# Another order for VectorE's and ScalarE's work at the entries of the two feed-forward blocks

## The chip, the core and the metric

The kernel runs on one core of a Trainium2 chip. Five engines of the core take their instructions in order, each from its own queue: TensorE (PE in the profile; its weight loads are PEld), VectorE (DVE), ScalarE (ACT), GpSimd (POOL) and SyncE (SP). The metric is the device time of one execution in microseconds (us); the time of a kernel is the median of its timed runs.

## The reference

The reference is a decoder trunk of two layers over 1024 positions of width 1024, in fp32. Layer 0 is a gated short convolution and a SwiGLU feed-forward block; layer 1 is a dilated attention and a second SwiGLU block. Each block is normalised ahead and added to the residual stream:

```
for i in range(DEPTH):
    h = rms_norm(x, mix_norm[i])
    x = x + (short_conv_mixer if i % 2 == 0 else dilated_attention_mixer)(h, ...)
    h = rms_norm(x, ffn_norm[i])
    x = x + (silu(h @ w_gate[i]) * (h @ w_up[i])) @ w_down[i]      # D_FF = 2816
return rms_norm(x, final_norm)
```

The change is about the place where a feed-forward block begins: the norm's statistics (mean of squares, root, reciprocal), the scaled input h, and the first of the products with `w_gate` and `w_up`.

## The kernel before

**Tiles.** The stream is held as 8 tiles X[n] of 128 rows (features) by 1024 columns (positions). Every fp32 operand of a matmul is split into a high part (a copy on ScalarE to fp32r) and a low part (a subtraction on VectorE (L140 for weights, L568 for inputs)), and a product is three matmuls: high by high, high by low, low by high (L575, L576, L577).

**Units and products.** In `Swiglu` a unit u is a pair of weight tiles: even units are gate columns, odd units up columns. Each unit is computed by seven Strassen-Winograd products m = 1, 2, 6, 7, 4, 5, 3, written (u, m) here. A product is 4 k-tiles of 3 matmuls, 12 in all, each of 512 columns. `unit_order` writes the order of the products out by hand. In the second feed-forward block (`key` is 1) it begins, with the place n of each in that list:

```
n:  0 (0,1)  1 (1,1)  2 (2,1)  3 (3,1)  4 (0,2)  5 (1,2)  6 (2,2)  7 (3,2)  8 (4,1)  9 (4,2)
   10 (0,6) 11 (1,6) 12 (0,7) 13 (1,7) 14 (0,4) 15 (1,4) 16 (0,5) 17 (1,5) 18 (0,3) 19 (1,3)
   20 (2,6) 21 (2,5) 22 (2,7) 23 (3,6) 24 (2,4) 25 (2,3) 26 (3,7) 27 (3,5) 28 (3,4) 29 (3,3)
```

In the first block (`key` is 0) it begins (0,1) (1,1) (0,2) (1,2) (2,1) (2,2) (3,1) (3,2) (0,6) (1,6) (0,7) (1,7) (0,4) (1,4) (0,5) (1,5) (0,3) (1,3) (2,6) (2,5) (2,7), n = 0 to 20.

**Banks.** The PSUM pool has 8 banks. A unit's products 1, 6, 7, 4 add up in bank p; product 2 goes to bank q, products 5 and 3 to bank r. After products 1, 6 and 7 `save` copies p to SBUF on ScalarE (L581). `first(u)` adds q to the saved product 1 on VectorE (L585), which ends q's use. Product 4 ends p's use: its result goes straight to `out`. `out` is a Silu on ScalarE for a gate quarter (L1239) and a multiplication on VectorE for an up quarter (L1242). When all four quarters of a pair of units are there, `store` makes four further sums on VectorE (L749), one for each later product.

**Inputs.** b[m] are the four k-tiles of the input for product m, each a page of high and low part. b[1] and b[2] come from `first_half`, made ahead of the block from the left half of the columns. The others come from the right half in `second_half`, a generator that is advanced at given places n: t3 (scale by the norm's factor `rstd`) and b[7]; then t2 = t3 + f and b[6]; then f[4..7] -= t2; then b[4], and h is scaled; then f[0..3] = h - t2; then b[5]; then b[3]. The norm's statistics for the right half are a generator, too: `stats` first issues 8 small matmuls (L485), a root on ScalarE (L488), a reciprocal and a diagonal tile on VectorE (L494), and on its next step two matmuls that spread the factor (L501) and a copy of it on ScalarE (L502).

**Order.** What stands in the program first stands first in its engine's queue. `take` and `ensure` make the weights' parts (L139 copy, L140 subtraction) two products ahead; `ensure(self.at(u, m))` makes them up to that product at once. The weights of products 6, 7, 5 and 3 are sums of raw weight tiles on VectorE (`combos`, L191). SBUF is a pool of 41 pages and one of 20 half pages; a tile that is asked for when none is free waits for the last reader of an earlier one. `feed_forward` runs `start(n)` behind each product n; that is the place where most of the change is.

**Before, in the second block:** n = 0: the last low part of b[2]. n = 1: `combos` of unit 1 and weights up to (0,6). n = 2: statistics, weight (1,6). n = 4: spread, t3, b[7] high parts, the Silu table, weights (0,7) and (1,7). n = 5: `first(0)`, `first(1)`, t2, b[6], low parts of b[7]. n = 6: f[4..7]. n = 11: b[4], h. n = 12: f[0..3]. n = 13: b[5]. n = 16: b[3]. Behind (1,3), n = 19, the first quarters of units 0 to 3 go to `out` together.

Of the kernel before, what the change touches and what calls it, by code (L numbers as in the profile page):

```python
# [13 lines left out]
ALU = mybir.AluOpType  # L14
# [7 lines left out]
KT = D // 128  # L22
# [73 lines left out]
def trunk(ctx: ExitStack, tc: tile.TileContext, x, gains_in, cwi, ck, cwo, wqkv, wo, relb,  # L96
# [444 lines left out]
    class Strassen:  # L541
# [75 lines left out]
        def whole(self, u, m, d):  # L617

            if m == 1:
                d["p"] = self.bank()  # L620
            elif m in (2, 5):
                d["q" if m == 2 else "r"] = self.bank()
            self.mm((u,), m, d["q" if m == 2 else "r" if m in (5, 3) else "p"], m in (1, 2, 5))
            if m in (1, 6, 7):
                d[{1: "u1", 6: "u2", 7: "u3"}[m]] = self.save(d["p"])
            if (u, m) == (0, 6):
                self.first(0)
            if m == 4:
                self.out(u, (1, 0), d.pop("p"))
            elif m == 3:  # L630
                self.out(u, (0, 1), self.add(d.pop("u2"), d.pop("r")))
            elif m in (5, 7) and "u3" in d and "r" in d:
                self.out(u, (1, 1), self.add(d.pop("u3"), d["r"]))
            early = self.key != 0
            if m == 2 and u > 3 + early or (u, m) in ((1, 3) if self.key == 1 else (0, 4), (3, 7)):
                for x in {u * (u < 2): range(4), 3: (4,) * early}.get(u, (u,)):
                    self.out(x, (0, 0), self.first(x))
                    del self.st[x]["u1"]

        def shallow(self, u, m, d):  # L640

# [504 lines left out]
    class Swiglu(Strassen):  # L1146
# [27 lines left out]
        def gained(self, n):  # L1174
# [6 lines left out]
            if n > 3:  # L1181
                self.xd[n - 4] = self.xg[n - 4]
                nc.gpsimd.dma_start(out=self.xd[n - 4], in_=t, accum_op=ALU.add)

        def second_half(self):

            tt = lambda out, a, b, op: nc.vector.tensor_tensor(out=out, in0=a, in1=b, op=op)
            rstd = self.norm.rstd[:, half(1)]
            t3, h, f = self.xd, {k: self.xg[4 + k] for k in range(4)}, self.f
            t2 = {k: X[4 + k][:, half(1)] for k in range(4)}  # L1190
            low7, low = [], None
            for k in range(4):
                tt(t3[k], t3[k], rstd, ALU.mult)
                low7.append(self.hi(7, k, t3[k]))
            if self.key:
                yield
                self.first(0)
                self.first(1)
            for k in range(4):
                tt(t2[k], t3[k], f[k], ALU.add)  # L1200
                nxt = self.hi(6, k, t2[k])
                if low:
                    low()
                low = nxt
            low7.pop(0)()
            low()
            for lo in low7:
                lo()
            yield

            for k in range(4):
                tt(f[4 + k], f[4 + k], t2[k], ALU.subtract)
            yield
            lows = [self.hi(4, k, f[4 + k]) for k in range(4)]
            if self.key:
                for lo in lows:
                    lo()
                lows = []
            for k in range(4):
                tt(h[k], h[k], rstd, ALU.mult)  # L1220
            for lo in lows:
                lo()
            yield
            for k in range(4):
                tt(f[k], h[k], t2[k], ALU.subtract)
            yield
            lows = [self.hi(5, k, f[k]) for k in range(4)]
            for lo in lows:
                lo()
            yield  # L1230
            lows = [self.hi(3, k, h[k]) for k in range(4)]
            for lo in lows:
                lo()
            X[:] = [None] * KT
# [12 lines left out]
        def feed_forward(self, stats, last_step, after, final=None):  # L1247
            prep = []

            def start(n):  # L1250
                if n == 0:
                    last_step()
                    if not self.key:
                        for m in (6, 7):
                            combos[self.key, 1](m)
                        ensure(self.at(3, 1))
                if n == 1 + self.key:
                    next(stats)
                if n == 1:
                    if self.key:  # L1260
                        for m in (6, 7):
                            combos[self.key, 1](m)
                    ensure(self.at(0, 6))
                if n == 2 + 2 * self.key:
                    run(stats)
                    prep.append(self.second_half())
                    next(prep[0])
                    nc.scalar.activation(scratch, eps, AF.Silu)
                if n == 2:
                    ensure(self.at(1, 6))  # L1270
                elif n == 4:
                    ensure(self.at(1, 7))
                if n in ((5, 7, 8, 9, 11), (5, 6, 11, 12, 13, 16))[self.key]:
                    ensure(self.base + n + 3)
                    next(prep[0], None)

            self.run(start)
            key = ("d", self.key)
# [28 lines left out]
    def into_ffn(i, norm):  # L1307
# [49 lines left out]
                       3 if key == "ao" else 4, added=added)  # L1357

        def last_step():
            run(pre[0])  # L1360
            norm.flush()

        return sw, group1, norm.stats(HALF, S), last_step

# [629 lines left out]
```

## Time and profile before

| | |
|---|---|
| time, median of 3 runs | 2137.87 us (2137.76 to 2138.27) |
| the profiled execution | 2138.59 us; span from first to last instruction 2136.8 us |
| granted TensorE clock | 0.998 of full speed |
| TensorE busy | 2117.3 us, 99% of the span |
| VectorE busy | 1718.8 us, 80% |
| ScalarE busy | 992.4 us, 46% |
| GpSimd busy | 221.9 us, 10% |
| first products of the first feed-forward block | from 331.05 us |
| first products of the second feed-forward block | from 1484.73 us |

Times in the traces count from the first instruction of the span. A row of the view of instructions in time order gives the start, the duration, engine, line, operation, tiles and count, and in brackets the idle time of that engine just before, with what ended it. A row of the view of waits gives the waiting engine and line, what it waited for, the total in us, the number of times and the longest. A row of the view by windows gives the window, its length, and for each engine the busy time and the number of instructions. A matmul's shown duration overlaps the next one's, since matmuls are pipelined: two that follow at once start less than one duration apart.

### The profile page before, as it was taken

To read this page: it belongs to the slowest core of one execution; us is meant where nothing else is said; L and a number is where in the kernel's file an instruction comes from. 1 tells how busy PE (TensorE), PEld (TensorE's weight loads), DVE (VectorE), ACT (ScalarE), POOL (GpSimd) and SP (SyncE) were. 2 spreads that over 40 slices of the span, in tenths; PEclk is the share of its full clock that TensorE was granted. 3 is DMA by queue.
4 is the path that set the end of the run, shared out by engine and by line. 5 is a ranking of instruction groups with operands and counts; after the bars stand their busy time and mean duration, and the time that the engine had idled before them with its cause. 6 is when DMAs were issued, how large, how long until landed. Compare 5 with 4: busy or idle time off the path is not lost.

```text
span 2136.8 us, 30748 instructions
## 1 busy us (share of the span) xinstructions
PE 2117.3 (99%) x11086; PEld 1815.5 (85%) x11086; DVE 1718.8 (80%) x3160; ACT 992.4 (46%) x1782; POOL 221.9 (10%) x316
## 2 busy tenths in 40 slices
PE   9999999999999999999999999999999999999998
PEld 7788888888888888878999999888788888888887
DVE  8898769888888888864676767768888888878876
ACT  7433336444544443344545454536544544444435
POOL 2000001111212000010111111110011212100000
PEclk9999999999999999999999999999999999999999
DMA  7222643334545784342333333635125545586432
GB/s 214 69 94 69 237 143 88 124 123 161 180 153 170 262 305 152 108 135 65 88 102 97 103 98 95 205 123 188 33 81 174 168 153 180 172 338 199 156 94 80
DMA packets 149347, 308.82 MB, mean 145 GB/s; under 512 B 50106, under 2 KB 61386, under 8 KB 149194
## 3 DMA queue, kind: packets, MB, share of 16 engines
q1 hardware_dynamic: 83306, 208.92, 30.6%
q0 software_dynamic: 25872, 79.02, 10.5%
q10 hardware_dynamic: 40016, 18.90, 3.0%
q8 instruction: 88, 1.44, 0.3%
q14 instruction: 65, 0.53, 0.1%
HBM read 209.06 MB, written 88.28 MB: 139 GB/s over the span
## 4 chain that ended last, share of the span: by engine, by line
PE 77%; issue 10%; DVE 7%; DMA 3%; ACT 2%; POOL 0%; SPq 0%; DVEq 0%; ACTq 0%; POOLq 0%
PE bank L575 16%; PE bank L577 16%; PE bank L576 16%; PE bank L1584 4%; PE bank L371 4%; PE bank L369 4%; PE bank L370 4%; PE bank L670 2%; PE bank L673 2%; PE bank L672 2%; PE bank L1444 1%; PE bank L1443 1%; PE bank L1442 1%; PE bank L1509 1%; PE bank L1508 1%
## 5 line engine op out<-in xcount | busy, mean ns | idle before, releaser
L575 PE MATMUL bank<-b,w 128*128 128x512 f32 x1816 | 710.0, 391 | 3.8 <-ACT w L139 2.2
L577 PE MATMUL bank<-b,w 128*128 128x512 f32 x1816 | 707.0, 389 | 2.1 <-DVE w L140 2.1
L576 PE MATMUL bank<-b,w 128*128 128x512 f32 x1816 | 707.7, 390 | 0.6 <-DVE b L568 0.3
L575 PEld LDWEIGHTS bank<-b,w 128*128 128x128 f32 x1816 | 341.1, 188 | 77.4 <-ACT w L139 5.2
L577 PEld LDWEIGHTS bank<-b,w 128*128 128x128 f32 x1816 | 341.0, 188 | 74.6 <-DVE w L140 3.4
L576 PEld LDWEIGHTS bank<-b,w 128*128 128x128 f32 x1816 | 341.2, 188 | 71.2 <-DVE b L916 1.1
L139 ACT ACTIVATE w<-combo 128x512 fp32r<-128x512 f32 (+2 forms) x448 | 229.3, 540 | 249.6 <-DVE combo L191 229.7
L140 DVE TENSOR_TENSOR w<-combo,w 128x512 fp32r<-128x512 f32 (+2 forms) x448 | 254.7, 581 | 30.8 <-ACT w L139 30.5
L581 ACT ACTIVATE part<-bank 128x512 f32<-128x512 f32 x168 | 100.2, 597 | 295.9 <-PE bank L577 292.2
L140 DVE TENSOR_TENSOR w<-raw,w 128x512 fp32r<-128x512 f32 (+2 forms) x308 | 169.4, 568 | 23.3 <-ACT w L139 23.1
L585 DVE TENSOR_TENSOR part<-part,bank 128x256 f32<-128x256 f32 (+1 forms) x328 | 154.2, 500 | 35.4 <-ACT part L581 20.0
L139 ACT ACTIVATE w<-raw 128x512 fp32r<-128x512 f32 (+2 forms) x308 | 150.9, 527 | 63.8 <-DMA raw<-in_ffn_w_down 19.1
L831 DVE TENSOR_TENSOR x<-x,bank 128x512 f32<-128x512 f32 x168 | 114.7, 683 | 37.2 <-PE bank L577 34.6
L369 PE MATMUL bank<-w_hi,w 128*128 128x512 f32 (+1 forms) x320 | 119.6, 374 | 0.0
L371 PE MATMUL bank<-w_hi,w 128*128 128x512 f32 (+1 forms) x320 | 117.8, 368 | 0.3 <-DVE w L140 0.3
L370 PE MATMUL bank<-w_lo,w 128*128 128x512 f32 (+1 forms) x320 | 117.7, 368 | 0.0
L506 DVE TENSOR_TENSOR x<-x,bank 128x512 f32<-128x512 f32 (+1 forms) x104 | 66.0, 642 | 56.0 <-PE bank L371 47.0
L369 PE MATMUL bank<-h_hi,w_hi 128*128 128x512 f32 x256 | 104.4, 408 | 0.0
L191 DVE TENSOR_TENSOR combo<-raw 128x512 f32<-128x512 f32 (+1 forms) x160 | 103.2, 645 | 0.0
L371 PE MATMUL bank<-h_hi,w_lo 128*128 128x512 f32 x256 | 100.0, 391 | 0.2 <-DVE w_lo L140 0.2
L370 PE MATMUL bank<-h_lo,w_hi 128*128 128x512 f32 x256 | 99.9, 390 | 0.0
L1603 ACT ACTIVATE z<-bank 64x512 f32<-64x512 f32 x32 | 19.0, 594 | 160.6 <-PE bank L1584 160.4
(266 smaller groups left out, 3816.7 us busy)
## 6 DMA issues: line engine op xcount, KB each, us to landing
hin<-part SPq DMA_DIRECT2D x126, 256.0 KB
raw<-in_ffn_w_gate SPq DMA_DIRECT2D x44, 512.0 KB
raw<-in_ffn_w_up SPq DMA_DIRECT2D x44, 512.0 KB
b<-ready SPq DMA_DIRECT2D x42, 512.0 KB
part<-sum POOLq DMA_DIRECT2D x72, 256.0 KB, 3.5
raw<-in_ffn_w_down SPq DMA_DIRECT2D x48, 384.0 KB
x<-spill SPq DMA_DIRECT2D x24, 512.0 KB
raw<-in_attn_w_qkv SPq DMA_DIRECT2D x24, 512.0 KB
```

What stands on the lines that cost most here:

```text
L139: nc.scalar.activation(hi, src, AF.Copy)
L140: eng.tensor_tensor(out=lo, in0=src, in1=hi, op=ALU.subtract)
L191: eng.tensor_tensor(out=c, in0=a, in1=b, op=op)
L369: nc.tensor.matmul(b, whi[:, a], ahi[:, s], start=first, stop=False)
L370: nc.tensor.matmul(b, whi[:, a], alo[:, s], start=False, stop=False)
L371: nc.tensor.matmul(b, wlo[:, a], ahi[:, s], start=False, stop=last)
L575: nc.tensor.matmul(b, hi[:, a], bhi, start=start and k == 0, stop=False, skip_group_check=True)
L576: nc.tensor.matmul(b, hi[:, a], blo, start=False, stop=False, skip_group_check=True)
L577: nc.tensor.matmul(b, lo[:, a], bhi, start=False, stop=k == n - 1, skip_group_check=True)
L581: nc.scalar.activation(t, b, AF.Copy)
L585: nc.vector.tensor_tensor(out=t, in0=t, in1=b, op=ALU.add)
L831: nc.vector.tensor_tensor(out=X[n][:, half(h)], in0=X[n][:, half(h)], in1=b, op=ALU.add)
```

## The change

In `whole`, unit 0, 1 and 2 of the second block no longer save product 1 right behind it; `start(2)` saves the three together. The first quarters go to `out` in pairs in both feed-forward blocks: those of units 0 and 1 behind (0,4), those of units 2 and 3 behind (2,5); before, all four went behind (1,3) in the second block and behind (0,4) in the first.

In the second block nothing is done at n = 1 any more. At n = 2 the statistics come first, then the three saves, the `combos` of unit 1 and the weights up to (4,2). The spread, t3 and the high parts of b[7] come at n = 3. A new generator `second_later` does the rest: n = 4 `first(0)` and t2; n = 5 `first(1)`, the low parts of b[7], and then the weights (0,6) and (1,6); n = 6 b[6], f[4..7], the scaling of h, and then the weights (0,7) and (1,7); n = 7 f[0..3]; n = 11 b[4]; n = 13 b[5]; n = 15 the high parts of b[3] and two of its low parts; n = 16 the other two.

In `into_ffn`, `last_step` adds the last square to the norm's sum ahead of the last low part of b[2], where it did so behind it. (In the second block that sum is already complete there, so this touches the first block alone.)

No operation is added or removed, and no shape changes.

```diff
--- before.py
+++ after.py
@@ -621,7 +621,7 @@
             elif m in (2, 5):
                 d["q" if m == 2 else "r"] = self.bank()
             self.mm((u,), m, d["q" if m == 2 else "r" if m in (5, 3) else "p"], m in (1, 2, 5))
-            if m in (1, 6, 7):
+            if m in (6, 7) or m == 1 and not (self.key == 1 and u < 3):
                 d[{1: "u1", 6: "u2", 7: "u3"}[m]] = self.save(d["p"])
             if (u, m) == (0, 6):
                 self.first(0)
@@ -632,10 +632,12 @@
             elif m in (5, 7) and "u3" in d and "r" in d:
                 self.out(u, (1, 1), self.add(d.pop("u3"), d["r"]))
             early = self.key != 0
-            if m == 2 and u > 3 + early or (u, m) in ((1, 3) if self.key == 1 else (0, 4), (3, 7)):
-                for x in {u * (u < 2): range(4), 3: (4,) * early}.get(u, (u,)):
-                    self.out(x, (0, 0), self.first(x))
-                    del self.st[x]["u1"]
+            done = {(0, 4): range(4), (3, 7): (4,) * early}
+            if self.key != CONV:
+                done.update({(0, 4): (0, 1), (2, 5): (2, 3)})
+            for x in (u,) if m == 2 and u > 3 + early else done.get((u, m), ()):
+                self.out(x, (0, 0), self.first(x))
+                del self.st[x]["u1"]
 
         def shallow(self, u, m, d):
 
@@ -1182,6 +1184,41 @@
                 self.xd[n - 4] = self.xg[n - 4]
                 nc.gpsimd.dma_start(out=self.xd[n - 4], in_=t, accum_op=ALU.add)
 
+        def second_later(self, low7, t3, t2, h, f, rstd, tt):
+
+            def operand(m, x):
+                for lo in [self.hi(m, k, x[k]) for k in range(4)]:
+                    lo()
+
+            self.first(0)
+            for k in range(4):
+                tt(t2[k], t3[k], f[k], ALU.add)
+            yield
+            self.first(1)
+            for lo in low7:
+                lo()
+            yield
+            operand(6, t2)
+            for k in range(4):
+                tt(f[4 + k], f[4 + k], t2[k], ALU.subtract)
+            for k in range(4):
+                tt(h[k], h[k], rstd, ALU.mult)
+            yield
+            for k in range(4):
+                tt(f[k], h[k], t2[k], ALU.subtract)
+            yield
+            operand(4, {k: f[4 + k] for k in range(4)})
+            yield
+            operand(5, f)
+            yield
+            lows = [self.hi(3, k, h[k]) for k in range(4)]
+            for lo in lows[:2]:
+                lo()
+            yield
+            for lo in lows[2:]:
+                lo()
+            X[:] = [None] * KT
+
         def second_half(self):
 
             tt = lambda out, a, b, op: nc.vector.tensor_tensor(out=out, in0=a, in1=b, op=op)
@@ -1194,8 +1231,8 @@
                 low7.append(self.hi(7, k, t3[k]))
             if self.key:
                 yield
-                self.first(0)
-                self.first(1)
+                yield from self.second_later(low7, t3, t2, h, f, rstd, tt)
+                return
             for k in range(4):
                 tt(t2[k], t3[k], f[k], ALU.add)
                 nxt = self.hi(6, k, t2[k])
@@ -1212,10 +1249,6 @@
                 tt(f[4 + k], f[4 + k], t2[k], ALU.subtract)
             yield
             lows = [self.hi(4, k, f[4 + k]) for k in range(4)]
-            if self.key:
-                for lo in lows:
-                    lo()
-                lows = []
             for k in range(4):
                 tt(h[k], h[k], rstd, ALU.mult)
             for lo in lows:
@@ -1256,23 +1289,29 @@
                         ensure(self.at(3, 1))
                 if n == 1 + self.key:
                     next(stats)
-                if n == 1:
+                if n == 1 + self.key:
                     if self.key:
+                        for u in range(3):
+                            self.st[u]["u1"] = self.save(self.st[u]["p"])
                         for m in (6, 7):
                             combos[self.key, 1](m)
-                    ensure(self.at(0, 6))
-                if n == 2 + 2 * self.key:
+                        ensure(self.at(4, 2))
+                    else:
+                        ensure(self.at(0, 6))
+                if n == 2 + self.key:
                     run(stats)
                     prep.append(self.second_half())
                     next(prep[0])
                     nc.scalar.activation(scratch, eps, AF.Silu)
-                if n == 2:
+                if n == 2 and not self.key:
                     ensure(self.at(1, 6))
-                elif n == 4:
+                elif n == 4 and not self.key:
                     ensure(self.at(1, 7))
-                if n in ((5, 7, 8, 9, 11), (5, 6, 11, 12, 13, 16))[self.key]:
+                if n in ((5, 7, 8, 9, 11), (4, 5, 6, 7, 11, 13, 15, 16))[self.key]:
                     ensure(self.base + n + 3)
                     next(prep[0], None)
+                if self.key and n in (5, 6):
+                    ensure(self.at(1, n + 1))
 
             self.run(start)
             key = ("d", self.key)
@@ -1357,8 +1396,8 @@
                        3 if key == "ao" else 4, added=added)
 
         def last_step():
+            norm.flush()
             run(pre[0])
-            norm.flush()
 
         return sw, group1, norm.stats(HALF, S), last_step
 
```

## The prediction

> **What bounds the kernel now.** I read four views: the page's busy times, the waits of TensorE at the two entries, the windows, and then the instructions in time order around each wait. The page's first part:
>
> ```profile
> PE 2117.3 (99%) x11086; PEld 1815.5 (85%) x11086; DVE 1718.8 (80%) x3160; ACT 992.4 (46%) x1782; POOL 221.9 (10%) x316
> ```
>
> TensorE sets the end, and the change takes no matmul away. It can only shorten stops of TensorE. The waits of TensorE from 1493 to 1560 us (second block), then from 330 to 400 us (first block), and two windows of the second block:
>
> ```profile
> PE bank L577 <- DVE w L140: 1.3, 1, 1.3
> PE bank L501 <- DVE diag L494: 0.8, 1, 0.8
> PE bank L575 <- DVE gate L1242: 0.7, 1, 0.7
> PE bank L575 <- ACT b L567: 0.4, 1, 0.4
> PE bank L576 <- DVE b L568: 0.3, 1, 0.3
> PE bank L575 <- ACT gate L1239: 0.2, 1, 0.2
> ...
> PE bank L577 <- DVE w L140: 0.7, 1, 0.7
> PE bank L485 <- DVE acc L470: 0.4, 1, 0.4
> ...
> 1484.70:1576.40 91.70, 88.01 (x384) 70.73 (x383) 83.88 (x142) 49.22 (x88) 8.91 (x14) 1.00 0.28 91
> 1527.00:1553.00 26.00, 23.15 (x97) 17.66 (x96) 25.14 (x42) 12.47 (x23) 2.77 (x5) 1.00 0.12 51
> ```
>
> Six stops in the second entry, 91.70 - 88.01 = 3.69 us of idle time; two in the first, 0.7 + 0.4 = 1.1. A window's row gives its length and then the busy time of PE, PEld, DVE, ACT and POOL: VectorE has 83.88 of 91.70, and 25.14 of 26.00 in the middle. So VectorE's queue decides what is late, and TensorE what that costs.
>
> Idle time is not the whole loss, as starts show. Two products' first matmuls, and the stop inside (2,7):
>
> ```profile
> 1484.73 0.39 PE L575 MATMUL bank<-b,w 128*128 128x512 f32 x1
> ...
> 1487.46 0.40 PE L575 MATMUL bank<-b,w 128*128 128x512 f32 x1
> ...
> 1550.55 0.39 PE L576 MATMUL bank<-b,w 128*128 128x512 f32 x1
> 1552.20 0.50 PE L577 MATMUL bank<-b,w 128*128 128x512 f32 x1 [1.27 <-DVE w L140]
> 1552.54 0.39 PE L575 MATMUL bank<-b,w 128*128 128x512 f32 x1
> ```
>
> Twelve matmuls take 2.73 us, so 0.227 from start to start, though each is shown as 0.39. Around the stop the starts are 1.65 and 0.34 apart: 1.42 + 0.11 = 1.53 lost, where 1.27 is shown idle. I add 0.26 to every stop: 3.69 + 6 x 0.26 = **5.25 us** in the second entry.
>
> The busy share alone would put the most there is to gain at 3.69 + 1.1 = 4.8 us. The Trainium skill, page "Trainium Kernel Development and Optimization", section "Performance Expectations", calls matmul busy time a bad measure because matmuls are pipelined; the rows above agree (0.39 shown, 0.227 apart). By idle time alone the gain below would be 4.5 us, by starts it is 6.4.
>
> **The change, stop by stop.** No instruction comes or goes, so each term is a stop that ends or moves. I walk ScalarE's and VectorE's queues in the new order, each with its pitch from rows: VectorE 0.60 (a x4 group below takes 2.49, its first result 0.69), ScalarE 0.52, a product 2.72. The same walk in the old order meets the trace's six stops within 0.3 us each.
>
> *The spread.* Statistics, ScalarE's queue ahead of the root, and the diagonal tile:
>
> ```profile
> 1492.91 0.94 PE L485 MATMUL bank<-ones,acc 128*128 128x1 f32 x8
> 1493.72 0.49 PE L575 MATMUL bank<-b,w 128*128 128x512 f32 x1
> ...
> 1493.68 0.71 ACT L1179 ACTIVATE x<-x,gains 128x512 f32<-128x512 f32 x1
> 1494.30 1.06 ACT L581 ACTIVATE part<-bank 128x512 f32<-128x512 f32 x2
> 1495.25 2.19 ACT L139 ACTIVATE w<-raw 128x512 fp32r<-128x512 f32 x4
> 1498.33 0.27 ACT L488 ACTIVATE r<-bank,eps 128x4 f32<-128x4 f32 x1
> ...
> 1499.56 0.69 DVE L494 TENSOR_TENSOR diag<-eye,r 128x512 f32<-128x512 f32 x1
> ```
>
> The sums are there at 1493.85, but the root stands behind saves and weight copies until 1498.33. In the new order it is next on ScalarE, at 1494.3; VectorE has only one low part ahead, so the diagonal tile is done at about 1495.5. TensorE asks for it behind (3,1), at 1493.72 + 2.72 = 1496.4: 0.9 to spare. The 0.8 stop goes. The three saves and four weight copies come behind the root; the first of those weights, for (2,2), is ready at 1498.0 and wanted at 1502.9.
>
> *The two r banks.* Products (0,5) and (1,5) wait for the banks that (0,4) and (1,4) leave:
>
> ```profile
> 1528.54 2.50 ACT L567 ACTIVATE b<-hcol 128x512 fp32r<-128x512 f32 x4 [1.40 <-DVE hcol L1187]
> 1530.94 0.58 ACT L1239 ACTIVATE gate<-bank 128x512 f32<-128x512 f32 x1
> ...
> 1530.83 2.49 DVE L568 TENSOR_TENSOR b<-hcol,b 128x512 fp32r<-128x512 f32 x4
> 1534.44 0.69 DVE L1242 TENSOR_TENSOR gate<-bank,gate 128x512 f32<-128x512 f32 x1
> ```
>
> The Silu stands behind b[5]'s copies, which wait for f on VectorE; the multiplication stands behind b[5]'s low parts. In the new order h is scaled at n = 6 and f made at n = 7, some 8 us sooner, so b[5]'s copies start at 1526.0 as soon as the weight ahead of them. The Silu runs when (0,4) ends, at 1528.0, and frees the bank at 1528.6, wanted at 1530.1. On VectorE b[5] is done at 1529.1; the moved multiplication of unit 1's first quarter, a `combo` and a weight go ahead, and the gate multiplication runs from 1531.1 to 1531.8, wanted at 1532.8. Both stops go, with 1.5 and 1.0 to spare.
>
> *b[3], for (0,3):*
>
> ```profile
> 1538.02 2.18 ACT L567 ACTIVATE b<-x 128x512 fp32r<-128x512 f32 x4
> ...
> 1538.77 2.49 DVE L568 TENSOR_TENSOR b<-x,b 128x512 fp32r<-128x512 f32 x4
> ```
>
> The copies stood behind a Silu that waited for VectorE. One place sooner (n = 15) they run from 1531.2 to 1534.8. Two low parts follow at 1532.9 and 1533.5; the other two stand behind an add of (0,5), two sums and a weight, at 1536.7 and 1537.3. (0,3) would start at 1535.5 and ask for the third low part at 1535.5 + 2 x 0.68 + 0.23 = 1537.1; it is there at 1537.4. Of the two stops one of 0.35 stays, with its tail 0.45.
>
> *The pairs of quarters, for (2,7):*
>
> ```profile
> 1547.54 1.28 DVE L585 TENSOR_TENSOR part<-part,bank 128x512 f32<-128x512 f32 x2
> 1548.92 0.69 DVE L1242 TENSOR_TENSOR part<-part 128x512 f32<-128x512 f32 x1
> ...
> 1551.46 0.69 DVE L140 TENSOR_TENSOR w<-combo,w 128x512 fp32r<-128x512 f32 x1
> ```
>
> (2,7)'s weight stood behind these three and one more multiplication. Now those of units 0 and 1 are over by (0,4), those of 2 and 3 come behind (2,5), after this weight. Its low part runs from 1545.8 to 1546.5, wanted at 1547.3: 0.8 to spare. The moved work delays (2,4)'s weight, done at 1551.6, wanted at 1552.7, and (2,3)'s, done at 1555.3, wanted at 1555.45. **That last 0.15 is what is late next.** Saving units 0 to 2 together costs nothing: their banks p stay in use until product 4 anyway.
>
> *The first block.* The stops are the sum of squares and (1,5)'s weight:
>
> ```profile
> 335.74 0.69 DVE L568 TENSOR_TENSOR b<-hcol,b 128x512 fp32r<-128x512 f32 x1 [0.16 <-ACT b L567]
> 336.35 0.69 DVE L470 TENSOR_TENSOR acc<-acc,sq 128x512 f32<-128x512 f32 x1
> ...
> 372.40 1.28 DVE L585 TENSOR_TENSOR part<-part,bank 128x512 f32<-128x512 f32 x2
> ...
> 374.99 0.68 DVE L140 TENSOR_TENSOR w<-combo,w 128x512 fp32r<-128x512 f32 x1
> ...
> 392.78 0.69 DVE L585 TENSOR_TENSOR part<-part,bank 128x512 f32<-128x512 f32 x1 [1.34 <-ACT part L581]
> ```
>
> With the sum ahead of the low part, TensorE starts the statistics 0.6 sooner: the stop's 0.4 and the 0.16 by which a shown duration passes a pitch (0.39 - 0.227). The diagonal tile there then comes about as TensorE asks for it. Units 2 and 3's adds and multiplication, from 372.40 to 374.39, leave the place ahead of (1,5)'s weight, which is then ready at 373.7, wanted at 374.2. That stop was 0.7 + 0.26 = 0.96. Together **1.6 us**; the three moved operations now stand behind (2,5), where VectorE idles 1.34 us; without that cover an add that no product waits for is 1.9 instead of 0.6 us late.
>
> **Sum.** 5.25 - 0.45 + 1.6 = 6.4 us. The profiled execution took 2138.59 (span 2136.8 and 1.8 around it) and would take 2132.2; it lies 0.7 above the median, 2137.87, so I forecast 2137.87 - 6.4 = **2131.5 us**. The most that can go is 5.25 + 1.6 and a few tenths of uncounted tails, 7.2: 2130.7.
>
> **Rivals.**
>
> *B, a page wait.* b[3] now asks for four pages while the weights of (1,4), (0,5), (1,5) and (0,3) are all alive. I count 24 pages of b, 4 of X, 8 raw weights and those 4: 40 of 41. The second to fourth copies must wait for a reader. Before, that happened at b[6]:
>
> ```profile
> 1514.99 0.63 ACT L567 ACTIVATE b<-x 128x512 fp32r<-128x512 f32 x1 [1.75 <-DVE b L568]
> ```
>
> My walk lets them go with (1,4)'s end and the first two low parts. If they must wait for (1,5)'s end at 1535.6, the next Silu, the weights of (1,3) and (2,6) and VectorE's low parts queue behind: the stop at (0,3) is 1.8 (fourth copy alone) to 3.1 us (from the second on) instead of 0.35, and the time 2133.0 to 2134.2. For it: every page is taken. Against it: earlier readers end in time. In the Trainium skill, "TensorE: Matmul & The Clock Gate", section "Architectural detail", ScalarE's queue is strictly first in, first out, so one waiting copy holds all behind it; the wait of 1.75 above, with nothing overtaking, agrees.
>
> *C, VectorE becomes the bound.* The margins are 0.15 to 1.0, and VectorE idles 0.86 of 26 us in the crowded stretch. Each us that it runs behind my walk from (0,3) on is a us of TensorE. At 2.1, three or four operations, the gain is down to 4.3. I give 2133.6 to 2137. Against it: the old order came out right by the same walk.
>
> *D, slower.* t3 needs accumulating DMAs, and stands ahead of `first(0)` on VectorE:
>
> ```profile
> L1183 POOL DMA_DIRECT2D x<-x x4: 842/850/882, 1487.8 to 1494.7; - x4
> ...
> DMA to landing us min/median/max: 6.9/7.6/8.5
> ```
>
> The last lands at 1494.7 + 6.9 = 1501.6, just when the new order asks for it; the old one asked 2 us later. If landings slip, VectorE holds `first(0)`, which frees the bank that (4,1) takes. That is wanted at 1508.3 and due at 1502.3, so 6 us are hidden, then each costs one; beyond 12.4 us the kernel is slower than before, 2139.5 at 14. Against it: 8.5 is the longest landing.
>
> **Chances.** Forecast 0.60 (2130.7 to 2132.4), B 0.20, C 0.14, D 0.06. What can be told from no change is about 0.2%, 4.3 us: 2133.6. Faster takes the forecast and most of B, 0.76; the same, the rest of B and most of C, 0.18; slower, D, 0.06. The range, 2130.6 to 2134.5, holds the forecast, B and a little of C.
>
> **What would show it.** Right: between 1493 and 1500 no wait of L501 for the diagonal tile; no wait of L575 for L1239 or L1242; no stop in (2,7); one short wait for L568 near 1537; the first block without waits for L470 and L140. (3,6) and what follows start some 6.4 us sooner against the span's start. Wrong: a b<-x copy on ScalarE idle for a us or more near 1532 to 1536 (B); new waits of L577 for L140 at (2,7) to (3,7) (C); VectorE idle at t3 for a DMA (D).

## The result and the profile after

The changed kernel takes **2130.56 us** (median of 6 runs, 2128.91 to 2131.29), the kernel before, timed beside it, 2138.07 (6 runs): 7.5 us less, ratio 0.9964 (95% interval 0.9954 to 0.9974). The forecast was 2131.5 with a range from 2130.6; the time lies 0.04 us below that range, with three of the six runs inside it. The profiled execution took 2130.26 us, its span is 2128.5.

TensorE's work is the same to the instruction, as the counts behind the x in the profile after show:

```profile
PE 2114.2 (99%) x11086; PEld 1815.6 (85%) x11086; DVE 1718.4 (81%) x3160; ACT 991.4 (47%) x1782; POOL 221.8 (10%) x316
```

What went is best read from windows that begin and end at the same matmul in both kernels. Each begins at the first product of a block and is called the block's entry here. The kernel before (window, its length, then busy time and count of PE, PEld, DVE, ACT, POOL; the granted clock; the DMA share and GB/s):

```profile
331.02:401.44 70.42, 69.30 (x305) 56.14 (x304) 66.05 (x112) 38.62 (x68) 6.10 (x10) 1.00 0.31 94
1484.76:1576.40 91.64, 87.95 (x384) 70.70 (x383) 83.82 (x142) 49.16 (x88) 8.91 (x14) 1.00 0.28 91
```

and the changed kernel:

```profile
331.04:399.65 68.61, 68.61 (x305) 56.39 (x304) 65.85 (x111) 38.31 (x68) 6.07 (x10) 1.00 0.33 97
1482.20:1568.70 86.50, 86.50 (x384) 70.94 (x383) 83.23 (x141) 48.82 (x88) 8.88 (x14) 1.00 0.30 96
1524.00:1550.00 26.00, 26.00 (x115) 21.12 (x114) 25.11 (x43) 13.19 (x24) 3.83 (x7) 1.00 0.14 56
```

The same 305 matmuls of the first block take 70.42 - 68.61 = **1.81 us** less, the same 384 of the second 91.64 - 86.50 = **5.14 us** less. (The prediction's window of the second entry, 91.70 us, begins 0.03 us ahead of the first matmul, the two of that entry here 0.03 behind it.) In all three windows after, TensorE is shown busy from end to end. Its busy time fell by 87.95 - 86.50 = 1.45 us in the second entry though no matmul went, so a part of the stops was shown as busy time. VectorE still has 25.11 of 26.00 us in the crowded stretch: it does the same work, in an order that shows no idle time of TensorE.

ScalarE of the changed kernel in time order, at the spread, and then at the Silu that frees an r bank and at b[3]:

```profile
1491.75 0.24 ACT L488 ACTIVATE r<-bank,eps 128x4 f32<-128x4 f32 x1
1491.89 1.56 ACT L581 ACTIVATE part<-bank 128x512 f32<-128x512 f32 x3
...
1525.41 0.59 ACT L1272 ACTIVATE gate<-bank 128x512 f32<-128x512 f32 x1
...
1528.47 0.61 ACT L567 ACTIVATE b<-x 128x512 fp32r<-128x512 f32 x1
1529.68 0.63 ACT L567 ACTIVATE b<-x 128x512 fp32r<-128x512 f32 x1 [0.59 <-DVE combo L191]
1530.53 1.15 ACT L567 ACTIVATE b<-x 128x512 fp32r<-128x512 f32 x2 [0.22 <-PE bank L577]
```

VectorE of the same kernel, from the spread to the pair of quarters:

```profile
1492.23 0.69 DVE L494 TENSOR_TENSOR diag<-eye,r 128x512 f32<-128x512 f32 x1
...
1528.36 0.68 DVE L1275 TENSOR_TENSOR gate<-bank,gate 128x512 f32<-128x512 f32 x1
...
1533.90 1.28 DVE L568 TENSOR_TENSOR b<-x,b 128x512 fp32r<-128x512 f32 x2
...
1542.92 0.69 DVE L140 TENSOR_TENSOR w<-combo,w 128x512 fp32r<-128x512 f32 x1
...
1544.72 1.28 DVE L585 TENSOR_TENSOR part<-part,bank 128x512 f32<-128x512 f32 x2
```

The root is the first thing on ScalarE behind the statistics, the three saves (L581) follow it. The pair of additions (L585) now stands behind (2,7)'s weight (L140 at 1542.92). b[3]'s second and third copies each wait a little (0.59 and 0.22), and its last two low parts come at 1533.90. That is where the one trace of a stop is left, inside (0,3):

```profile
1534.35 0.39 PE L575 MATMUL bank<-b,w 128*128 128x512 f32 x1
1534.64 0.50 PE L576 MATMUL bank<-b,w 128*128 128x512 f32 x1
1534.97 0.39 PE L577 MATMUL bank<-b,w 128*128 128x512 f32 x1
```

The starts are 0.29 and 0.33 us apart where 0.227 is the pitch (the time from start to start when nothing is awaited), and no idle time is shown: a stop of less than 0.39 - 0.227 = 0.16 us is hidden in the shown duration of the matmul ahead of it.

### The profile page after: what moved, and what is told of

It is laid out like the page before. It is cut to its first block, busy times and chain, and to the rows that moved or that the text cites. A ratio compares the mean times of both kernels' runs of the same rounds, so it can differ in the third digit from the quotient of the medians.

```text
span 2128.5 us, 30749 instructions
## 1 busy us (share of the span) xinstructions
PE 2114.2 (99%) x11086; PEld 1815.6 (85%) x11086; DVE 1718.4 (81%) x3160; ACT 991.4 (47%) x1782; POOL 221.8 (10%) x316
## 3 DMA queue, kind: packets, MB, share of 16 engines
q8 instruction: 88, 1.44, 0.3%
## 4 chain that ended last, share of the span: by engine, by line
PE 95%; DVE 3%; ACT 1%; issue 1%; DMA 0%; DVEq 0%; ACTq 0%
PE bank L575 19%; PE bank L576 19%; PE bank L577 19%; PE bank L371 6%; PE bank L369 6%; PE bank L370 6%; PE bank L1623 5%; PE bank L672 2%; PE bank L675 2%; PE bank L674 2%; PE bank L1483 1%; PE bank L1482 1%; PE bank L1481 1%; PE bank L1548 1%; PE bank L1547 1%
## 5 line engine op out<-in xcount | busy, mean ns | idle before, releaser
L140 DVE TENSOR_TENSOR w<-combo,w 128x512 fp32r<-128x512 f32 (+2 forms) x448 | 254.4, 581 | 29.7 <-ACT w L139 29.5
L581 ACT ACTIVATE part<-bank 128x512 f32<-128x512 f32 x168 | 100.1, 597 | 295.4 <-PE bank L577 290.4
L140 DVE TENSOR_TENSOR w<-raw,w 128x512 fp32r<-128x512 f32 (+2 forms) x308 | 169.2, 568 | 22.8 <-ACT w L139 22.6
L585 DVE TENSOR_TENSOR part<-part,bank 128x256 f32<-128x256 f32 (+1 forms) x328 | 154.1, 500 | 33.3 <-ACT part L581 18.0
L191 DVE TENSOR_TENSOR combo<-raw 128x512 f32<-128x512 f32 (+1 forms) x160 | 103.1, 645 | 0.0
```

Source lines behind the costliest of these rows:

```text
L140: eng.tensor_tensor(out=lo, in0=src, in1=hi, op=ALU.subtract)
L191: eng.tensor_tensor(out=c, in0=a, in1=b, op=op)
L585: nc.vector.tensor_tensor(out=t, in0=t, in1=b, op=ALU.add)
```

## The experiments

In each profile the window that holds the same 384 matmuls of the second entry is quoted; its length is compared with the 86.50 us above. Each window begins and ends some 0.03 us behind the start of the same matmul, so that the length does not move with what happens elsewhere in the execution. "L" numbers are those of the kernel in question.

**The same kernels once more**, no edit.

> The changed kernel, not altered. Theory: the sum of the prediction was too small at its terms (1.8 us for the first block, 5.2 for the second by the starts of the first profiles), and what lies outside the two entries is variation between executions: the ratio to the kernel before is 0.9962 to 0.9970, 8.1 to 6.4 us, and in this profile the second entry is left with one stop of 0.2 to 0.4 us, while the stop of 757 us and the last transfers come out either way. Rival: the change also takes away work outside the entries; then the stop at 757 us is gone and the last transfers land some 9.7 us behind the last matmul here too.

> The kernel before, not altered, for a second profile. Theory: in the two entries the same stops as in the first profile within 0.3 us each (3.7 us idle from 1484 to 1577, 1.1 from 330 to 400); the stops elsewhere (0.26 us at 757 us, the start of the kernel, the last transfers at 10.5 us behind the last matmul) may come out otherwise, by some tenths of a us. Rival: they come out as in the first profile; then they belong to the old order and their loss is the change's.

Measured: the changed kernel 2130.43 (2130.15 to 2130.6), ratio 0.9965 (0.9951 to 0.9979); the kernel before as an experiment of its own 2137.09 (11 runs), beside 2137.72 (24 runs) for the very same kernel timed as the comparison: 0.63 us apart. The windows of the changed kernel:

```profile
331.26:399.87 68.61, 68.61 (x305) 56.38 (x304) 65.84 (x111) 38.32 (x68) 6.05 (x10) 1.00 0.32 97
1483.09:1569.57 86.48, 86.48 (x384) 70.94 (x383) 83.21 (x141) 48.81 (x88) 8.87 (x14) 1.00 0.30 96
```

The kernel before, the same two windows:

```profile
331.31:401.69 70.38, 69.28 (x305) 56.14 (x304) 66.04 (x112) 38.62 (x68) 6.09 (x10) 1.00 0.31 94
1483.95:1575.65 91.70, 87.93 (x384) 70.69 (x383) 83.83 (x142) 49.16 (x88) 8.90 (x14) 1.00 0.28 91
```

The entries repeat within 0.06 us (the second gives 91.70 - 86.48 = 5.22 this time), the rest does not. The stop for a raw weight near 757 us is in the first profile of before, not in the second; it is not in the first profile of the changed kernel, which has one near 1907 us instead, and is back in its second. The waits, each row with who waited for what, the total, times and longest; the kernel before, first profile, from 750 to 760 us:

```profile
PE bank L575 <- ACT w L139: 0.3, 1, 0.3
```

The changed kernel, first profile, from 1900 to 1918 us:

```profile
PE bank L575 <- ACT w L139: 0.6, 1, 0.6
```

The changed kernel, second profile, from 750 to 760 us:

```profile
PE bank L575 <- ACT w L139: 0.5, 1, 0.5
```

So these stops come and go in both orders, and the rival that the change takes them away falls. Behind the last matmul before had 8.2 and 8.0 us to the end of the span, the changed kernel 7.25 and 7.4, the first block's part alone 7.0. All twelve profiles of kernels with the change or a part of it lie between 6.9 and 7.5, so some 0.5 us or more may have gone there; whether that has to do with the order stays open.

**One block alone.** The first kernel is the kernel before with the first block's part only:

```
-            if m == 2 and u > 3 + early or (u, m) in ((1, 3) if self.key == 1 else (0, 4), (3, 7)):
-                for x in {u * (u < 2): range(4), 3: (4,) * early}.get(u, (u,)):
...
+            done = {(1, 3) if self.key == 1 else (0, 4): range(4), (3, 7): (4,) * early}
+            if self.key == 0:
+                done.update({(0, 4): (0, 1), (2, 5): (2, 3)})
...
         def last_step():
-            run(pre[0])
             norm.flush()
+            run(pre[0])
```

> Only the first block's part of the change, on the kernel before: the sum of squares ahead of the low part, and the quarters in pairs. Theory: 1.6 us (prediction) to 1.8 us (starts in the profile after) faster than before, ratio 0.9991 to 0.9993, with the second entry's six stops as before. Rival, that the first block's gain is lost again further on: ratio 1.0000.

The second is the changed kernel with these two put back:

```
-            if self.key != CONV:
+            if self.key == 1:
                 done.update({(0, 4): (0, 1), (2, 5): (2, 3)})
...
-            norm.flush()
             run(pre[0])
+            norm.flush()
```

> Only the second block's part of the change; the first block as before. Theory: 4.8 us (prediction) to 5.2 us (starts) faster than before, ratio 0.9976 to 0.9978, and with the other part alone it adds up to the whole change within 0.5 us. Rival, that the two parts need each other or that the second block gives more than its own stops: 6 us or more, ratio 0.9972 or less.

Measured: 2134.64 (ratio 0.9986, 0.9977 to 0.9995) and 2131.98 (0.9973, 0.9963 to 0.9983). The first and second entry of the first block's part alone:

```profile
330.99:399.60 68.61, 68.61 (x305) 56.38 (x304) 65.86 (x111) 38.32 (x68) 6.07 (x10) 1.00 0.33 97
1482.04:1573.71 91.67, 87.94 (x384) 70.71 (x383) 83.85 (x142) 49.20 (x88) 8.90 (x14) 1.00 0.28 91
```

The second block's part alone:

```profile
330.99:401.39 70.40, 69.30 (x305) 56.14 (x304) 66.04 (x112) 38.63 (x68) 6.09 (x10) 1.00 0.32 94
1484.37:1570.90 86.53, 86.53 (x384) 70.95 (x383) 83.11 (x141) 48.84 (x88) 8.86 (x14) 1.00 0.30 96
```

By the windows the parts are independent: the first gives 70.42 - 68.61 = 1.81 and leaves the second entry at 91.67, the second gives 91.64 - 86.53 = 5.11 and leaves the first at 70.40. The medians give 3.1 and 5.7, whose sum, 8.8, misses the whole, 7.3, by more than the 0.5 us expected. With 0.6 us between two timings of one kernel, and intervals of 2 us on each side, a part of this size cannot be sized by medians.

**The root back behind its queue**, the spread left early. The diff is against the changed kernel, second block:

```
-                    next(stats)
-                if n == 1 + self.key:
                     if self.key:
                         for u in range(3):
...
                         ensure(self.at(4, 2))
-                    else:
+                    next(stats)
+                    if not self.key:
                         ensure(self.at(0, 6))
```

> The changed kernel, with the root, its reciprocal and the diagonal tile of the second block put back behind the three saves, the two sums of products and the four weights, while the spread stays asked for one product sooner. Theory of the prediction: the root starts behind 3 saves of 0.48 and 4 copies of 0.52, about 3.5 us later than now, the diagonal tile is done near 1499 us on the axis of before and wanted at 1496.4: one stop of 2.4 to 3.0 us at L501, and 2.6 to 3.3 us slower than the changed kernel (2133.0 to 2133.8). Rival, that the early root matters little because later slack takes the delay up: under 1 us.

Measured: 2134.58 us (2132.33 to 2135.71; 0.9987, 0.9978 to 0.9996). The first matmul of the spread, in time order:

```profile
1497.05 1.22 PE L501 MATMUL bank<-diag,ones 128*128 128x512 f32 x1 [3.02 <-DVE diag L494]
```

The entry and three windows across the stop:

```profile
1482.05:1574.57 92.52, 89.50 (x384) 72.59 (x383) 83.25 (x141) 49.07 (x88) 8.85 (x14) 0.96 0.28 90
...
1495.00:1495.98 0.98, 0.00 (x0) 0.00 (x0) 0.98 (x2) 0.84 (x3) 0.00 (x0) 1.00 1.09 238
1495.98:1502.81 6.83, 5.76 (x12) 3.90 (x13) 3.48 (x7) 2.89 (x5) 0.00 (x0) 0.50 0.25 48
1502.81:1505.00 2.19, 2.19 (x11) 1.79 (x10) 1.31 (x3) 2.16 (x5) 0.00 (x0) 1.00 0.00 0
```

The stop came at the place and in the size expected, 3.0 us. The loss did not: 92.52 - 86.50 = 6.0 us, twice the expected 2.6 to 3.3. The windows show why: while TensorE stood, its granted clock fell to 0.50 at 1495.98, 1.95 us into the idle time (1497.05 - 3.02 = 1494.03), and came back at 1502.81, 5.76 us after work had begun again. So the place of the root alone decides over the spread's stop, the rival falls, and this stop costs about twice its length. Beside the kernel before (2137.18) the median is 2.6 us less, where the unaltered changed kernel has 7.3: 4.7 us lost. The ten runs lie 3.4 us apart; whether all lost as much to the clock as the profiled one is not shown.

**The scalings back** (h behind b[4]'s low parts, f just ahead of b[5]):

```
                 tt(f[4 + k], f[4 + k], t2[k], ALU.subtract)
+            yield
+            yield
+            operand(4, {k: f[4 + k] for k in range(4)})
             for k in range(4):
                 tt(h[k], h[k], rstd, ALU.mult)
...
                 tt(f[k], h[k], t2[k], ALU.subtract)
-            yield
-            operand(4, {k: f[4 + k] for k in range(4)})
-            yield
             operand(5, f)
```

> The changed kernel, with h scaled again behind b[4]'s low parts and f made again just ahead of b[5]. Theory: the bank stops come back, 0.4 us at (0,5) and 1.4 at (1,5), and the stop inside (0,3) grows to 1.2: about 2.8 us slower than the changed kernel (2133.2). Rival, that the pages or VectorE as a whole bind and the place of the scalings does not: no stop at (0,5) and (1,5), under 0.5 us.

The entry's window:

```profile
1482.76:1572.16 89.40, 87.44 (x384) 70.73 (x383) 82.96 (x141) 49.17 (x88) 8.85 (x14) 1.00 0.29 94
```

Its waits of TensorE there:

```profile
PE bank L575 <- ACT gate L1272: 0.7, 1, 0.7
PE bank L575 <- ACT b L567: 0.7, 1, 0.7
PE bank L576 <- DVE b L568: 0.6, 1, 0.6
```

2132.64 us; the entry is 2.90 longer (expected 2.8), with the three stops at the three places named; they share the loss more evenly than expected (0.7 at (0,5) and at (1,5) instead of 0.4 and 1.4, and 0.6 shown inside (0,3) instead of 1.2). The moved scalings are thus what cleared both r banks and most of (0,3).

**Three moves undone one at a time:** the quarters in one place behind (1,3); the spread one product later; b[3] all at n = 16.

```
-            if self.key != CONV:
+            if self.key == 1:
+                done = {(1, 3): range(4), (3, 7): (4,)}
+            elif self.key != CONV:
                 done.update({(0, 4): (0, 1), (2, 5): (2, 3)})
```

```
-                if n == 2 + self.key:
+                if n == 2 + 2 * self.key:
                     run(stats)
```

```
             operand(5, f)
             yield
-            lows = [self.hi(3, k, h[k]) for k in range(4)]
-            for lo in lows[:2]:
-                lo()
             yield
-            for lo in lows[2:]:
+            lows = [self.hi(3, k, h[k]) for k in range(4)]
+            for lo in lows:
                 lo()
```

> The changed kernel, with the second block's four quarters again in one place behind (1,3). Theory: (2,7)'s weight comes 2.5 us later on VectorE, of which 1.0 is slack: one stop of 1.4 to 1.6 us for that weight at (2,7) and 1.1 us slower in all, since a small stop at (0,3) goes (2131.6). Rival: under 0.4 us, if the other moves have already made enough room.

> The changed kernel, with the spread and the t3 products one product later, as in the kernel before; the root stays ahead. Theory: the root's place alone takes the stop away, and what follows has the room; no stop of L501, within 0.3 us of the changed kernel (2130.2 to 2130.8). Rival: the earlier spread is what gives the later operands their room; new stops of 0.5 us or more at (0,6) to (0,4).

> The changed kernel, with all of b[3] made one place later, as in the kernel before. Theory: the copies stand again behind the Silu of (0,5), and (0,3) stops for 0.6 us instead of 0.2 to 0.35: 0.3 us slower at most, too little for the time to tell; the profile shows a stop at L575 or L576 for b of 0.5 to 0.8 us. Rival: the stop is 1 us or more, as before (0.4 + 0.3 with tails 1.2).

The entry with the quarters back:

```profile
1482.59:1570.12 87.53, 86.51 (x384) 71.03 (x383) 83.80 (x142) 48.83 (x88) 8.88 (x14) 1.00 0.30 95
```

The spread later:

```profile
1483.95:1570.45 86.50, 86.50 (x384) 70.95 (x383) 83.05 (x141) 48.89 (x88) 8.87 (x14) 1.00 0.30 97
```

b[3] later:

```profile
1483.22:1570.05 86.83, 86.50 (x384) 71.04 (x383) 83.25 (x141) 48.45 (x88) 8.87 (x14) 1.00 0.30 96
```

They are 1.03, 0.00 and 0.33 us longer, against 1.1, 0 and up to 0.3 expected. The first stops 1.0 us for (2,7)'s weight (1.4 to 1.6 expected), the third 0.3 inside (0,3) (0.5 to 0.8 expected). The second shows that the earlier spread by itself brings nothing here. The medians are 2130.27, 2129.55 and 2130.21, which is 6.9, 7.6 and 7.2 us below the kernel before timed beside each; the unaltered changed kernel is 7.3 below. A loss of 1.03 us shows there as 0.4, one of 0.33 as 0.1, and none as a gain of 0.3: differences under 1 us stand in the windows alone. (In all three profiles the clock fell for 3.4 us near 937 us, far from these edits; the last section has it.) The place of the three saves was not undone by itself.

**Rival B, one page less.** A tile that is written and read once holds one page from n = 4 to n = 20 of the second block:

```
+                if self.key and n == 4:
+                    self.held = [page("held") for k in range(1)]
+                    for t in self.held:
+                        nc.gpsimd.memset(t[:, :8], 0.0)
+                if self.key and n == 20:
+                    for t in self.held:
+                        nc.gpsimd.tensor_copy(self.kept, t[:, :8])
+                    del self.held
```

> The changed kernel, with one page of the on-chip memory held by an extra tile from the fifth to the twenty-first product of the second block. Rival B of the prediction, that pages bind at b[3]: the copies of b[3] or b[5] wait for a reader, and a stop of 0.5 to 2.8 us at (0,3) or sooner shows. Theory (one page of 41 is free): the ScalarE copies wait somewhat longer and TensorE shows at most 0.3 us more.

The entry of this kernel:

```profile
1484.39:1571.77 87.38, 86.79 (x384) 70.87 (x383) 83.26 (x141) 48.95 (x88) 9.20 (x16) 1.00 0.29 96
```

ScalarE there, at b[3]:

```profile
1532.54 1.15 ACT L567 ACTIVATE b<-x 128x512 fp32r<-128x512 f32 x2 [1.44 <-DVE combo L191]
```

0.88 us longer, with a stop of 0.6 inside (0,3): more than the theory's 0.3, at the low end of rival B's 0.5 to 2.8. The first copy of b[3] now waits 1.44 us, until a `combo` on VectorE (L191) ends, for a page where in the changed kernel it was the second, for 0.59. The rival's mechanism is real and one page away; in the changed kernel it stays off TensorE's path. (The median, 2133.19, is higher than this explains; in this profile the first block's entry began at 332.0 us, in all others between 330.7 and 331.5, and took 0.5 us more than in the changed kernel; VectorE waited 2.5 us instead of 1.5 for accumulating transfers of the sums of squares (L470), shortly before and in it. The edit does not touch that place; why it happened there is not known.)

**Rival C, VectorE's room.** Additions of 128x64 on a small tile, ahead of b[3]'s last two low parts, 6 of them (shown) or 14:

```
+            for k in range(6):
+                tt(self.spare, self.spare, self.spare, ALU.add)
             for lo in lows[2:]:
                 lo()
```

> The changed kernel, with six small additions on VectorE (128x64, some 0.14 to 0.2 us each, about 1 us together) ahead of the last two low parts of b[3]. Theory: there is no slack on VectorE at (0,3): the stop inside (0,3) grows by the sum of the six, to 1.0 to 1.5 us, and what follows keeps its margin because TensorE is as much later. 0.8 to 1.2 us slower than the changed kernel. Rival: 0.5 us or more of it is taken up by slack.

> The same with fourteen additions (about 2.2 to 2.8 us). Theory: one stop of 2.2 to 3.0 us inside (0,3) and no other; 2.0 to 2.8 us slower than the changed kernel, linear with the six. Rival C of the prediction, that VectorE is the bound from there on: stops at (2,7), (2,4) or (2,3) too, and more than 3.2 us slower.

The entry with six:

```profile
1484.02:1571.94 87.92, 86.59 (x384) 70.94 (x383) 84.38 (x147) 48.76 (x88) 8.87 (x14) 1.00 0.29 94
```

VectorE there, the six and what follows:

```profile
1535.70 1.52 DVE L1229 TENSOR_TENSOR spare<-spare 128x64 f32<-128x64 f32 x6
1537.13 1.28 DVE L568 TENSOR_TENSOR b<-x,b 128x512 fp32r<-128x512 f32 x2
```

The low parts are 1537.13 - 1535.70 = 1.43 us later, and the entry is 1.42 us longer (somewhat over the expected 0.8 to 1.2, since one addition took 0.24 rather than 0.14 to 0.2). There is no slack at this place, and no other stop follows. With fourteen, the entry and two windows from the stop on:

```profile
1482.92:1574.21 91.29, 87.88 (x384) 72.07 (x383) 86.91 (x156) 48.98 (x88) 8.88 (x14) 0.98 0.29 92
...
1538.00:1538.44 0.44, 0.00 (x0) 0.00 (x0) 0.44 (x2) 0.00 (x0) 0.00 (x0) 1.00 0.00 0
1538.44:1541.86 3.42, 2.99 (x7) 2.42 (x8) 3.32 (x6) 0.00 (x0) 0.54 (x1) 0.50 0.00 0
```

4.79 us longer, over the 2.0 to 2.8 expected of the theory and over the 3.2 named for rival C. Yet rival C's sign, stops at (2,7), (2,4) or (2,3), is absent: the one stop inside (0,3) is 3.41 us long, since an addition took 0.25, and the clock fell again, at 1538.44, for 3.0 us of work, which makes up most of the rest (4.79 - 3.41 - 0.16 = 1.2). VectorE binds at (0,3) alone. The medians, 2131.75 and 2135.79, agree in direction (1.6 and 5.6 us lost, each against the kernel before beside it).

## Why the prediction was right and wrong

**The stops: right.** The signs it named are there: no wait for the diagonal tile, for the Silu or the gate multiplication, none in (2,7), none in the first block for L470 or L140. Only the short wait for L568 inside (0,3) is too short to be shown as one, and (3,6), named to start some 6.4 us sooner, starts 7.7 sooner in the first pair of profiles and 6.1 in the second. In times, too, the walk of the two queues holds. The second entry's axis after lies 2.55 us ahead of before's; shifted by that, the forecast has the diagonal tile done at 1492.95 (it is 1492.92), the Silu at 1525.45 (1525.41), the gate multiplication at 1528.55 (1528.36), b[3]'s first copy at 1528.65 (1528.47), its last low parts from 1534.15 (1533.90), (2,7)'s weight from 1543.25 (1542.92).

**The step that failed is the sum with its ceiling,** "The most that can go is 5.25 + 1.6 and a few tenths of uncounted tails, 7.2: 2130.7". The stops did not exceed that ceiling: the entries gave 6.95 us. It failed as the bound of a measured time, since the sum put all that lies outside the entries at nothing, without a reason. Two of its terms were small, and that third one missing:

- *The first block:* 1.6 predicted, 1.81 measured. By starts 0.5 of it went at the statistics, as priced, the rest at (1,5). The stop there was priced at its idle time and 0.26. But a second stop follows in that product that shows no idle at all. TensorE of the kernel before:

```profile
377.90 0.39 PE L577 MATMUL bank<-b,w 128*128 128x512 f32 x1
378.22 0.47 PE L575 MATMUL bank<-b,w 128*128 128x512 f32 x1
378.53 0.40 PE L576 MATMUL bank<-b,w 128*128 128x512 f32 x1
```

Starts 0.32 and 0.31 apart, 0.17 us over two pitches, with nothing in the brackets.

- *The second block:* 5.25 - 0.45 = 4.8 predicted, 5.14 measured (5.22 in the second pair of profiles). The stop that was to stay at (0,3), "with its tail 0.45", cost 0.18 there and 0.14 more at the start of the next product, 0.32 in all by the starts. What the six stops had cost was thus 5.14 + 0.32 = 5.46, where 3.69 + 6 x 0.26 = 5.25 was put: 0.30 beyond its idle time for each, instead of 0.26. (With the scalings put back, three stops of 0.69, 0.68 and 0.59 cost 2.90 + 0.32 in all, 0.42 each beyond their idle time, but that includes a delay at the start of (0,3) that shows no idle time.)

Together 6.95 us instead of 6.4. From the median used, 2137.87 - 6.95 = 2130.92, which would have lain inside the range.

- *Nothing outside the entries.* The measured 7.5 and 7.3 us are 0.6 and 0.3 more than the two entries give in the same pair of profiles. The forecast had no term for this, and its lower bound left it no room. Two timings of one kernel differ by 0.63 us, and stops for raw weights of 0.3 to 0.6 us come and go in both orders; that is enough for the difference, so it need not be the change's. How much of it is, stays open. (A fall of the clock near 937 us, 1.6 us in size, is in the profiles of four variants and in none of these two kernels' four; whether any of their other runs had it is not known.) That the median came to lie just below the edge, and not just above, was chance: of the six runs three lie on either side.

**The rivals.** B was put as "The second to fourth copies must wait for a reader". They did wait, for 0.81 us, and TensorE hardly noticed; with a page less it did. C asked for VectorE to run behind the walk; it ran ahead of it by 0.2 to 0.3 us. Of the narrow margins, (2,3)'s "last 0.15" held too. D, late landings of the accumulating transfers, was not tried on the chip. In the changed kernel t3 followed the weights at 1497.18, but the last transfer, issued at 1492.1, landed 6.9 us later at the soonest, at 1499.0, as the fourth of the scalings came up; the four took 2.59 us, in the kernel before 2.50. So D's landings came as just in time as it said, and its 6 us of room on TensorE's side were not touched.

## What to carry to other kernels

Where one engine sets the end and its stops are waits for results of other in-order queues, walk those queues in the new order with durations from the rows, and read both the stop and the gain from starts of the same instruction, since shown idle time misses every stop shorter than the pipelined overlap (0.16 us here). Do not set the edge of a range at the sum of the stops that one profile shows: leave it the spread between two timings of one kernel, 0.6 us here. A change of some tenths of a per cent is sized by equal-work windows of two profiles, which begin at the start of the same matmul, not by medians.

## What the hardware showed that was not expected

A stop of TensorE had two prices here. Up to the 1.3 us of the six additions the loss was the delay of the awaited result (1.42 for 1.43 us). At 3.0 and 3.4 us the granted clock fell to half within the stop, 1.95 us into the idle time in the one case and 2.98 in the other (1538.87 - 3.41 = 1535.46, and 1.00 until 1538.44), and stayed there for 5.76 and 2.99 us of work. From fall to return that is 6.83 and 3.42 us. Matmuls then started 0.427 us apart instead of 0.227. A stop of 1.5 to 1.6 us near 62 us, which every profile has, left the clock at 1.00, and none has a stop between that and 3.02 us, so where the second price begins is not shown. TensorE of the kernel with fourteen additions:

```profile
1538.87 0.80 PE L576 MATMUL bank<-b,w 128*128 128x512 f32 x1 [3.41 <-DVE b L568]
1539.46 0.63 PE L577 MATMUL bank<-b,w 128*128 128x512 f32 x1
1539.89 0.63 PE L575 MATMUL bank<-b,w 128*128 128x512 f32 x1
```

The Trainium skill, page "TensorE: Matmul & The Clock Gate", section "Part 1: The HAM clock gate (the "warmup" mystery)", describes this: the array's clock is halved once an activity window of about 3.4 us has passed idle, the window runs free of the kernel, and cold matmuls of 512 columns start 426.7 ns apart. The 0.427 agrees, and so do the times at half clock, once and twice 3.42 us; a clock that falls 1.95 us into a stop is sooner than a full idle window would have it.

In the prediction the price of a long stop concerns the rivals alone: B's upper case, a stop of 3.1 us, was priced without it, and would have been some 1 to 3 us worse by these two runs.

The clock also fell where TensorE did not stop. In four of the fourteen profiles (quarters back, spread later, b[3] later, fourteen additions) it stood at half for 3.4 us near 937 us, behind eight small matmuls of 33 x 16 that take 2.5 us; in the ten others the same eight left it at 1.00. No edit touches that place. The eight with b[3] later, and then the same window in that kernel and in the changed one:

```profile
934.80 2.59 PE L524 MATMUL bank<-oh,rel 33*16 33x512 f32 x8
...
938.00:941.00 3.00, 3.00 (x9) 2.33 (x8) 3.00 (x6) 1.09 (x1) 0.52 (x1) 0.50 0.33 63
...
938.00:941.00 3.00, 3.00 (x15) 2.48 (x14) 2.96 (x7) 0.87 (x1) 0.52 (x1) 1.00 0.33 57
```

The eleven starts behind the eight took 4.21 us (937.32 to 941.53) instead of 2.63 (937.10 to 939.73): 1.6 us that come and go from one execution to the next, more than most of the single moves above are worth.
